# Moving 280 stores and transfers from ScalarE's DMA queue to the sync engine's

## The chip, the cores and the metric

The kernel runs on one core of one Trainium2 chip. The metric is device time in microseconds (us) of one execution. A core has TensorE (PE, the matrix products), VectorE (DVE), ScalarE (ACT), GpSimd (POOL) and the sync engine (SP), each with its own stream of instructions, and 16 DMA engines that all streams share. A DMA is issued by an instruction in the stream of one of SP, ACT or POOL; that instruction waits, in its place in the stream, for whatever its data need, and what stands behind it in the stream waits too.

## The reference, cut to what matters

```python
def reference(x, p, ...):                       # x (1, 2048, 1024), p (1, 1, 2048, 256)
    z = rms_norm(x, mix_norm_g) @ w_in          # 1024 -> 26 * 128 columns
    y_conv = short_conv_mixer(z[..., :1536], conv_mix_w)
    y_rwkv = rwkv7_mixer(z[..., 1536:], ...)
    x = x + concatenate([y_conv, y_rwkv]) @ w_out
    x = x + conv_glu_ffn(rms_norm(x, ffn_norm_g), ...)      # 1024 -> 2 * 2816 -> 1024
    e = rms_norm(p @ ple_w_proj, ple_norm_g)
    gate = sigmoid(rms_norm(x, ple_gate_norm_g) @ ple_w_gate)
    return rms_norm(x + gate * e, final_norm_g)

def wkv7_scan(r, w, k, v, kk, a):               # per head, S is 64 x 64
    # S_t = S_{t-1} diag(w_t) + (S_{t-1} (-kk_t)) (kk_t*a_t)^T + v_t k_t^T,  out_t = S_t r_t
```

The recurrence of `wkv7_scan` runs over all 2048 frames. The kernel works it out by chunks of 64 frames, and for each chunk a unit lower triangular matrix has to be inverted, which is called the solve below.

## The kernel before

Time is cut into four groups (g) of 512 frames. First come the input projections of all four groups, to about 720 us; then for each group the output projection (o), the ConvFFN (up with line 417 behind it, down with line 457), the embedding (e, `ple_embed`, in the middle of the up products) and the gate products, with the final norm of the group behind the first rows of the next. Each product is made of three matmuls of split halves (hi and lo) over blocks of 128 x 512, accumulated in three PSUM buffers.

A weight comes from the host as raw float32 (`raw`, issued by SP) only once. ACT writes its hi half (line 153), POOL its lo half (line 154), and SP stores the split pair to DRAM (line 171, names k..., such as ku). Later groups load the kept pair by a DMA that POOL issues (line 161). There are four buffers for split pairs (whl...), so a load is issued just when a pair has been used up.

The time mixer (RWKV) runs beside the products as 16 units (u = 0 to 15) of 128 frames each: a generator that a product step advances by one. TensorE's instructions keep the order in which the program writes them; the other engines' orders, and SP's, are set by a scheduler that simulates the program and puts ready instructions in the order of its clock, with priority for some. A unit's input is z of its frames: the projections store it to `zs` (line 308) and the unit loads it from there (tw, ad, gd, k, v, r, lines 563 to 568, on SP). A solve has these steps: DVE transposes the triangular blocks into `ltt` (line 763); four DMAs store them to a DRAM tile `ld` (768); four DMAs read them back in another layout into `lm` (775), where each waits for all of `ld`; DVE folds two rows into one (`fold`, lines 783 to 786); POOL clears two diagonals (787, 788); DVE does 16 steps of substitution (794, 798); one DMA stores the result to `xd` (803); four DMAs read it into `dt` (810); DVE transposes it into `dn` (814), POOL copies it into `tT` (821, `tt` in the profile). TensorE uses `dn` first in `gm_ps`, some twenty product steps after the solve began. `xs` is loaded with the identity for the solve (790).

Other transfers: y, e, p, x and xr are rows that SP loads (line 203); the conv's result goes to `ys` at line 336, the unit's at line 931, e to `es` at line 371, and the output at line 519. The buffers u, yc, e, o and others share one pool with six buffers (`buf`, tag b); a buffer is free when the store from it has landed. All DMAs that SP and ACT issue share eight completion semaphores in turn.

Of the kernel before, what the change touches and what calls it, by code (L numbers as in the profile page):

```python
# [62 lines left out]
def tile_trunk(  # L63
# [18 lines left out]
    nc = tc.nc  # L82
# [37 lines left out]
    def v(name, i, n=1):  # L120
        o, _ = VEC[name]
        return vec[:, o + i : o + i + n]
# [25 lines left out]
    zs = [dram.tile([P, 14, G], F32, tag=f"zs{g}", name=f"zs{g}") for g in range(NG)]  # L148
    ys = [dram.tile([P, 8, G], F32, tag=f"ys{g}", name=f"ys{g}") for g in range(NG)]
    es = [dram.tile([P, 8, G], F32, tag=f"es{g}", name=f"es{g}") for g in range(NG)]  # L150
# [26 lines left out]
    def weight(pools, src, name):  # L177
        return [
            half(pools, src[:, 512 * c : 512 * c + 512], f"{name}_{c}", f"{name}_{c}")
            for c in range(2)  # L180
        ]

    def quad(pools, src, mp, name):
        cols = slice(256 * mp, 256 * mp + 256)
        return [half(pools, src[:, :, cols].rearrange("j p c -> p j c"), name, name)]
# [12 lines left out]
    def buf(pools, name):  # L198
        return pools["tmp"].tile([P, G], F32, tag="b", name=name, bufs=NBUF)
# [53 lines left out]
    def scaled(pools, ps, rstd, halo, pad):  # L253
        zb = pools["tmp"].tile([P, G + 2], F32, tag="zb", name="zb")
        nc.vector.tensor_tensor(out=zb[:, 2 : G + 2], in0=ps, in1=rstd, op=ALU.mult)  # L255
        nc.gpsimd.tensor_copy(zb[:, 2 - pad : 2], halo)
        nc.gpsimd.tensor_copy(halo, zb[:, G + 2 - pad : G + 2])
        return zb
# [10 lines left out]
    def product(pools, w, rows, evac):  # L269
        ps = pools["psd"].tile([P, G], F32, tag="d", name="ps_mm")  # L270
        for k in range(KD):
            mm3(ps, w, k, rows.hs[k], k == 0, k == KD - 1)
            if k == 3:
                yield
        if rows.ss is None or rows.scale is not None:
            with tc.high_priority():
                evac(ps, rows.scale)
        else:
            with tc.high_priority():
                raw = buf(pools, "raw")  # L280
                nc.scalar.copy(raw, ps)
            rows.held.append((raw, evac))
            if len(rows.held) == HELD:
                rows.scale = rows.ss.rstd(pools)
                with tc.high_priority():
                    for raw, evac in rows.held:
                        evac(raw, rows.scale)
        yield
# [6 lines left out]
    def in_proj(pools, g, rows, nxt):  # L295
        def project(m, evac):
            return product(pools, weight(pools, w_in[m], f"in{m}"), rows, evac)

        def lerp(j):
            def evac(ps, rstd):  # L300
                zb = scaled(pools, ps, rstd, z_last[:, j : j + 1], 1)
                u = buf(pools, "u")
                nc.scalar.activation(u, zb[:, 2 : G + 2], AF.Copy, scale=mu_c[:, j : j + 1])
                nc.vector.scalar_tensor_tensor(
                    out=u, in0=zb[:, 1 : G + 1], scalar=v("rwkv_mu", j), in1=u,
                    op0=ALU.mult, op1=ALU.add,
                )
                nc.scalar.dma_start(out=zs[g][:, j, :], in_=u)
            return evac

        for j in (12, 0, 4, 8, 13, 1, 5, 9, 2, 6, 10, 3, 7, 11):
            yield from project(12 + j, lerp(j))

        for i in range(4):
            st = {}

            def evac_x(ps, rstd):
                x = st["x"] = buf(pools, "xin")
                nc.vector.tensor_tensor(out=x, in0=ps, in1=rstd, op=ALU.mult)
                nc.vector.tensor_tensor(out=x, in0=x, in1=rstd, op=ALU.mult)  # L320

            def evac_c(ps, rstd):
                t = scaled(pools, ps, st["x"], cx_last[:, i, :], 2)
                u = st["c"] = buf(pools, "cu")
                nc.scalar.activation(u, t[:, 2 : G + 2], AF.Copy, scale=v("conv_mix_w", 8 + i))
                for d in (1, 0):
                    nc.vector.scalar_tensor_tensor(
                        out=u, in0=t[:, d : d + G], scalar=v("conv_mix_w", 4 * d + i), in1=u,
                        op0=ALU.mult, op1=ALU.add,
                    )  # L330

            def evac_b(ps, rstd):
                u = buf(pools, "yc")
                nc.vector.tensor_tensor(out=u, in0=ps, in1=rstd, op=ALU.mult)
                nc.vector.tensor_tensor(out=u, in0=u, in1=st["c"], op=ALU.mult)
                nc.scalar.dma_start(out=ys[g][:, i, :], in_=u)

            if i:
                nxt(3 * i - 3)
            yield from project(i, evac_x)  # L340
            if i:
                nxt(3 * i - 2)
            yield from project(8 + i, evac_c)
            if i:
                nxt(3 * i - 1)
            yield from project(4 + i, evac_b)

    def ple_rows(pools, g):
# [9 lines left out]
    def ple_embed(pools, g, st):  # L358
        hs = st
        ss = SumSq()  # L360
        for mp in range(KD // 2):
            w = quad(pools, w_proj, mp, f"pj{mp}")
            for mm in range(2):
                m = 2 * mp + mm
                ps = pools["psd"].tile([P, G], F32, tag="d", name="ps_e")
                for k in range(2):
                    mm3(ps, w, 2 * k + mm, hs[k], k == 0, k == 1)
                with tc.high_priority():
                    t = buf(pools, "e")
                    nc.scalar.copy(t, ps)  # L370
                    nc.scalar.dma_start(out=es[g][:, m, :], in_=t)
                ss.add(pools, t)
            yield
        embed[g] = ss
# [12 lines left out]
    def dense_rest(pools, g, yrows, nxt):  # L387
        tmp = pools["tmp"]
        gs = slice(g * G, (g + 1) * G)
# [120 lines left out]
        def finish():  # L510
            rstd = ss.rstd(pools)
            with tc.high_priority():
                for m in range(KD):
                    t = buf(pools, "o")
                    nc.vector.scalar_tensor_tensor(
                        out=t, in0=x2[m], scalar=v("final_norm_g", m), in1=rstd,
                        op0=ALU.mult, op1=ALU.mult,
                    )
                    nc.scalar.dma_start(out=out[m, :, gs], in_=t)

        pending.append(finish)

# [54 lines left out]
    def rwkv_unit(rp, S, u, loaded, following):  # L577
        pr, ch, ps_p, ps_c = rp["prep"], rp["chain"], rp["ps_p"], rp["ps_c"]
        g, off = u // 4, (u % 4) * P
        s = 0  # L580
        ts = slice(off, off + P)
# [16 lines left out]
        def r8(t):  # L598
            return t.rearrange("p (h n) -> p h n", h=8)
# [23 lines left out]
        for ct in range(4):  # L623
# [3 lines left out]
            out=ksum, in_=ps_n.rearrange("p (a h n) -> p a h n", a=4, h=2),  # L627
# [12 lines left out]
        for ct in range(4):  # L640
# [3 lines left out]
            out=mean, in_=r8(ps_v), op=ALU.add, axis=mybir.AxisListType.X  # L644
# [4 lines left out]
        for c in range(2):  # L649
            rs = slice(64 * c, 64 * c + 64)  # L650
            pair = []
            for par in range(2):
                t = ch.tile([P, 4, 64], F32, tag=f"suv{par}", name=f"suv{par}_{u}_{c}")
                vr = slice(64 - 64 * par, 128 - 64 * par)
                nc.vector.scalar_tensor_tensor(
                    out=t[vr], in0=mean4[rs, :, par, None].broadcast_to([64, 4, 64]),
# [29 lines left out]
        def cv(t):  # L686
# [9 lines left out]
            out=b_t, in0=tha, scalar=1.0, in1=kr, op0=ALU.add, op1=ALU.mult  # L696
        )
        b4 = cv(b_t)
        for rs, cs in ((E, lo), (O, hi)):
            nc.vector.scalar_tensor_tensor(  # L700
                out=bk[rs, :, :, cs], in0=b4[rs], scalar=0.5, in1=em[rs, :, :, 1:65],
# [63 lines left out]
        )  # L765
        for pq in range(4):
            q = pq % 2
            nc.scalar.dma_start(
                out=ld[pq].rearrange("c a i j -> i c a j"),
                in_=ltt[32 * pq : 32 * pq + 32, :, :, 32 * q : 32 * q + 32],  # L770
            )
        lm = ch.tile([P, 32, 32], F32, tag="lm", name=f"lm{u}", bufs=1)
        for r in range(4):
            eng = nc.sync if r % 2 else nc.scalar
            eng.dma_start(
                out=lm[r:P:4].rearrange("m i j -> m (i j)"),
                in_=ld.rearrange("q c a i j -> (q c a) (i j)"),
            )
# [12 lines left out]
        for i in range(0, 32, 2):  # L791
# [3 lines left out]
                out=pd[:, :, :, 0:n], in0=xs[:, :, None, 0:n].broadcast_to([P, 8, 2, n]),  # L795
# [3 lines left out]
                out=xs[:, :, i : i + 2], in_=pd[:, :, :, 0:n], op=ALU.add,  # L799
# [4 lines left out]
            out=xd.rearrange("q n r c i -> (q n r) (c i)"),  # L804
            in_=xs.rearrange("p c i -> p (c i)"),
        )
        dt_ = ch.tile([P, 8, 32], F32, tag="dt", name=f"dt{u}", bufs=1)
        for pq in range(4):
            eng = nc.sync if pq % 2 else nc.scalar
            eng.dma_start(  # L810
                out=dt_[32 * pq : 32 * pq + 32], in_=xd[pq].rearrange("n r c i -> (r c) n i")
            )
# [110 lines left out]
        yt = big("yt")  # L923
# [4 lines left out]
            )  # L928
        hi_tt(out=yt, in0=yt, in1=v_t, op=ALU.add)
        hi_tt(out=yt, in0=yt, in1=g_t, op=ALU.mult)  # L930
        nc.scalar.dma_start(out=ys[g][:, 4:8, ts], in_=yt)
        yield

    pools, rp = {}, {}
# [139 lines left out]
```

## Time and profile before

| | |
|---|---|
| median of 3 runs | 2907.62 us (2907.26 to 2908.49) |
| profiled execution | 2908.45 us, its span 2906.5 us |
| mean granted clock of TensorE | 0.984 of full speed |
| busy: PE, DVE, ACT, POOL | 2768.1, 1908.3, 959.9, 1117.4 us |
| DMA queue of POOL (q0), SP (q1), ACT (q10): share of 16 engines' span | 39.4%, 24.0%, 5.2% |

A busy time is the sum over the instructions of an engine; the share of the span that it leaves is idle, and the trace names for each idle time the instruction or the DMA whose end released it. An issue of a DMA (SPq, ACTq) isn't counted as busy, but the time that it takes and the time that it waits hold up what stands behind it on that engine. A row `[2.06 <-DMA whld<-kd]` behind an instruction says that its engine stood idle for 2.06 us before it and that the DMA from kd to whld released it.

### The profile page before, as it was taken

How to read it: one execution, taken by the hardware profiler on the slowest of the kernel's cores; microseconds unless marked ns; L12 is line 12 of the kernel's file. 1: busy time of each engine (PE TensorE's matmuls, PEld its weight loads, DVE VectorE, ACT ScalarE, POOL GpSimd, SP SyncE). 2: the span in 40 equal slices, each digit the busy share in tenths (PEclk: the TensorE clock that was granted, in tenths of full speed). 3: DMA queues.
4: the chain of work that ended last, by engine and by line, in shares of the span. 5: the costliest groups of instructions: out<-in, count | busy, mean ns of one | idle time of the engine just before them, and what ended most of it. 6: DMA issues, size and time to landing. Idle time of an engine off the chain costs nothing.

```text
span 2906.5 us, 42153 instructions
## 1 busy us (share of the span) xinstructions
PE 2768.1 (95%) x15464; PEld 2226.7 (77%) x15464; DVE 1908.3 (66%) x3039; ACT 959.9 (33%) x1721; POOL 1117.4 (38%) x1700
## 2 busy tenths in 40 slices
PE   8999999999889999989999999999999999999997
PEld 5778888778677877767778887777788877788885
DVE  5575665648587868796766676857676765544446
ACT  5332232312553433443412223434222143411113
POOL 4533232324556565652333333333333332433221
PEclk9999999999999999989999999999999999999998
DMA  8887777767777777767666565766565668666665
GB/s 298 297 261 217 236 214 223 209 210 243 263 252 245 258 241 247 248 228 230 178 186 185 173 192 172 233 202 200 174 192 169 187 187 266 216 195 189 196 188 169
DMA packets 285802, 629.95 MB, mean 217 GB/s; under 512 B 60186, under 2 KB 113690, under 8 KB 285596
## 3 DMA queue, kind: packets, MB, share of 16 engines
q0 software_dynamic: 95040, 346.07, 39.4%
q1 hardware_dynamic: 134144, 232.83, 24.0%
q10 hardware_dynamic: 56412, 48.36, 5.2%
q8 instruction: 122, 2.00, 0.3%
q14 instruction: 84, 0.69, 0.1%
HBM read 467.77 MB, written 159.38 MB: 216 GB/s over the span
## 4 chain that ended last, share of the span: by engine, by line
PE 50%; DVE 22%; DMA 14%; issue 6%; ACT 5%; POOL 3%; ACTq 1%; SPq 0%; DVEq 0%; POOLq 0%
PE ps_mm L86 33%; PE ps_d L86 11%; DVE uf L417 3%; DVE pd L794 3%; DVE xs L798 2%; DMA lm<-ld 1%; DMA xd<-xs 1%; DMA ld<-ltt 1%; DVE zb L255 1%; DVE sq L229 1%; DMA es<-e 1%; PE o_ps L86 1%; DMA dt<-xd 1%; DVE lo L215 1%; DMA x<-in_xT 1%
## 5 line engine op out<-in xcount | busy, mean ns | idle before, releaser
L86 PE MATMUL ps_mm<-hi,whlu 128*128 128x512 f32 x2816 | 910.6, 397 | 11.3 <-POOL whlu L154 5.1
L86 PEld LDWEIGHTS ps_mm<-hi,whlu 128*128 128x128 f32 x2816 | 532.3, 189 | 131.9 <-POOL whlu L154 7.8
L86 PE MATMUL ps_mm<-hi,whlin 128*128 128x512 f32 x1664 | 542.9, 400 | 19.6 <-ACT whlin L153 7.1
L86 PE MATMUL ps_mm<-lo,whlu 128*128 128x512 f32 x1408 | 552.3, 392 | 1.5 <-DVE lo L215 1.5
L86 PE MATMUL ps_d<-hi,whld 128*128 128x512 f32 x1408 | 456.1, 396 | 16.7 <-DMA whld<-kd 7.2
L86 PEld LDWEIGHTS ps_mm<-hi,whlin 128*128 128x128 f32 x1664 | 316.7, 190 | 93.0 <-ACT whlin L153 7.1
L417 DVE SCALAR_TENSOR_TENSOR uf<-zb,vec,uf 128x512 f32<-128x512 f32 x352 | 298.6, 851 | 89.6 <-ACT uf L412 78.4
L86 PE MATMUL ps_mm<-lo,whlin 128*128 128x512 f32 x832 | 328.9, 395 | 2.8 <-DVE lo L215 2.8
L412 ACT ACTIVATE uf<-zb,vec 128x512 f32<-128x512 f32 x176 | 143.1, 815 | 562.0 <-DVE zb L255 536.8
L86 PEld LDWEIGHTS ps_d<-hi,whld 128*128 128x128 f32 x1408 | 265.6, 189 | 79.2 <-DVE x L457 8.4
L86 PEld LDWEIGHTS ps_mm<-lo,whlu 128*128 128x128 f32 x1408 | 266.8, 189 | 56.2 <-DVE lo L215 2.4
L161 POOL DMA_DIRECT2D whlu<-ku x264 | 141.7, 537 | 436.8 <-PE ps_mm L86 289.1
L255 DVE TENSOR_TENSOR zb<-ps_mm,rstd 128x512 f32<-128x512 f32 x216 | 148.5, 688 | 208.0 <-PE ps_mm L86 204.4
L86 PE MATMUL ps_d<-lo,whld 128*128 128x512 f32 x704 | 275.4, 391 | 0.0
L457 DVE TENSOR_TENSOR x<-ps_d,x 128x512 f32<-128x512 f32 x192 | 131.6, 687 | 139.5 <-PE ps_d L86 138.7
L86 PEld LDWEIGHTS ps_mm<-lo,whlin 128*128 128x128 f32 x832 | 158.4, 190 | 38.1 <-DVE lo L215 6.6
L161 POOL DMA_DIRECT2D whlin<-kin x156 | 84.1, 539 | 248.9 <-PE ps_mm L86 207.7
L86 PE MATMUL ps_mm<-hi,whlg 128*128 128x512 f32 x512 | 169.2, 406 | 3.4 <-DMA whlg<-kg 3.4
L86 PE MATMUL ps_mm<-hi,whlo 128*128 128x512 f32 x512 | 163.1, 397 | 8.5 <-DMA whlo<-ko 4.9
L154 POOL TENSOR_TENSOR lo<-th,hi 128x512 fp32r<-128x512 f32 x88 | 115.2, 1310 | 110.9 <-ACT hi L153 110.3
L154 POOL TENSOR_TENSOR whlu<-rawu,whlu 128x512 fp32r<-128x512 f32 x88 | 122.6, 1398 | 88.9 <-ACT whlu L153 79.2
L86 PEld LDWEIGHTS ps_d<-lo,whld 128*128 128x128 f32 x704 | 133.2, 189 | 26.0
(205 smaller groups left out, 4248.0 us busy)
## 6 DMA issues: line engine op xcount, KB each, us to landing
whlu<-ku POOLq DMA_DIRECT2D x264, 512.0 KB, 4.5
whlin<-kin POOLq DMA_DIRECT2D x156, 512.0 KB, 4.8
whld<-kd POOLq DMA_DIRECT2D x132, 512.0 KB, 4.0
ku<-whlu SPq DMA_DIRECT2D x88, 512.0 KB, 4.7
kin<-whlin SPq DMA_DIRECT2D x52, 512.0 KB, 5.3
whlo<-ko POOLq DMA_DIRECT2D x48, 512.0 KB, 5.5
whlg<-kg POOLq DMA_DIRECT2D x48, 512.0 KB, 3.9
rawu<-in_w_up SPq DMA_DIRECT2D x88, 256.0 KB, 4.1
```

The source lines that it names most:

```text
L86: return pin(nc.tensor.matmul(*args, **kw))
L154: nc.gpsimd.tensor_tensor(out=lo, in0=raw, in1=hi.bitcast(F32), op=ALU.subtract)
L161: nc.gpsimd.dma_start(out=t, in_=kept[key])
L215: nc.vector.scalar_tensor_tensor(out=lo, in0=src, scalar=gcol, in1=hi.bitcast(F32), op0=ALU.mult, op1=ALU.subtract)
L229: nc.vector.tensor_tensor(out=sq, in0=sq, in1=self.acc, op=ALU.add)
L255: nc.vector.tensor_tensor(out=zb[:, 2 : G + 2], in0=ps, in1=rstd, op=ALU.mult)
L412: nc.scalar.activation(u, zb[:, 2 : G + 2], AF.Identity, bias=v("ffn_conv_b", n), scale=v("ffn_conv_w", 88 + n),)
L417: nc.vector.scalar_tensor_tensor(out=u, in0=zb[:, d : d + G], scalar=v("ffn_conv_w", 44 * d + n), in1=u, op0=ALU.mult, op1=ALU.add,)
L457: nc.vector.tensor_tensor(out=x2[m], in0=ps, in1=x2[m], op=ALU.add)
L794: tt(out=pd[:, :, :, 0:n], in0=xs[:, :, None, 0:n].broadcast_to([P, 8, 2, n]), in1=lm[:, None, i : i + 2, 0:n].broadcast_to([P, 8, 2, n]), ...
L798: nc.vector.tensor_reduce(out=xs[:, :, i : i + 2], in_=pd[:, :, :, 0:n], op=ALU.add, axis=mybir.AxisListType.X,)
```

## The change

Seven places of the kernel issue their DMAs from `nc.sync` instead of `nc.scalar`; nothing else is edited. Where the four transfers of `lm` and of `dt` alternated between the two engines, all four are SP's.

```diff
@@ lerp (zs), evac_b (ys), ple_embed (es), finish (out), end of a unit (ys)
-                nc.scalar.dma_start(out=zs[g][:, j, :], in_=u)
+                nc.sync.dma_start(out=zs[g][:, j, :], in_=u)
...
-                nc.scalar.dma_start(out=ys[g][:, i, :], in_=u)
+                nc.sync.dma_start(out=ys[g][:, i, :], in_=u)
...
-                    nc.scalar.dma_start(out=es[g][:, m, :], in_=t)
+                    nc.sync.dma_start(out=es[g][:, m, :], in_=t)
...
-                    nc.scalar.dma_start(out=out[m, :, gs], in_=t)
+                    nc.sync.dma_start(out=out[m, :, gs], in_=t)
...
-        nc.scalar.dma_start(out=ys[g][:, 4:8, ts], in_=yt)
+        nc.sync.dma_start(out=ys[g][:, 4:8, ts], in_=yt)
@@ the solve
         for pq in range(4):
             q = pq % 2
-            nc.scalar.dma_start(
+            nc.sync.dma_start(
                 out=ld[pq].rearrange("c a i j -> i c a j"),
...
         for r in range(4):
-            eng = nc.sync if r % 2 else nc.scalar
+            eng = nc.sync
             eng.dma_start(
                 out=lm[r:P:4].rearrange("m i j -> m (i j)"),
...
         for pq in range(4):
-            eng = nc.sync if pq % 2 else nc.scalar
+            eng = nc.sync
             eng.dma_start(
                 out=dt_[32 * pq : 32 * pq + 32], in_=xd[pq].rearrange("n r c i -> (r c) n i")
```

The scheduler then orders SP and ACT anew. TensorE's order stays, POOL's nearly so; DVE's moves by a few places within each solve. Three places follow.

In unit 7, where first-pass weights are still being split, ACT before the change has two `lm` transfers among its casts of weights (whlu18 is the pair of half 18, hi written from rawu18):

```order
L768 DMA ld7_10522<-ltt7_10523 32x8x32 x4
L153 CAST whlu18_0_10708<-rawu18_0_10709 128x512
L775 DMA lm7_10529<-ld7_10522 32x1024
L153 CAST whlu18_1_10715<-rawu18_1_10716 128x512
L775 DMA lm7_10529<-ld7_10522 32x1024
L153 CAST whlu40_0_10755<-rawu40_0_10756 128x512
```

and after it the casts alone:

```order
L757 COPY tok7_1_10499<-ps_k_10510 128x512
L153 CAST whlu18_0_10708<-rawu18_0_10709 128x512
L153 CAST whlu18_1_10715<-rawu18_1_10716 128x512
L153 CAST whlu40_0_10755<-rawu40_0_10756 128x512
L153 CAST whlu40_1_10762<-rawu40_1_10763 128x512
```

The casts moved up to the place where `ld7` and `lm7` stood. SP in the same place has before the change the two other `lm` transfers, and then raw loads and stores of kept pairs:

```order
L775 DMA lm7_10529<-ld7_10522 32x1024 x2
L168 DMA rawu19_0_10811<-in_w_up 128x512
L171 DMA ku18_0_10713<-whlu18_0_10708 128x1024
L168 DMA rawu19_1_10818<-in_w_up 128x512
L171 DMA ku18_1_10720<-whlu18_1_10715 128x1024
L168 DMA rawu41_0_10858<-in_w_up 128x512
```

and after it

```order
L768 DMA ld7_10522<-ltt7_10523 32x8x32 x4
L775 DMA lm7_10529<-ld7_10522 32x1024 x2
L168 DMA rawu19_0_10811<-in_w_up 128x512
L775 DMA lm7_10529<-ld7_10522 32x1024
L168 DMA rawu19_1_10818<-in_w_up 128x512
L775 DMA lm7_10529<-ld7_10522 32x1024
L171 DMA ku18_0_10713<-whlu18_0_10708 128x1024
L171 DMA ku18_1_10720<-whlu18_1_10715 128x1024
L168 DMA rawu41_0_10858<-in_w_up 128x512
```

Four `ld` and four `lm` stand in one row with two raw loads between the last three `lm`; the store ku18_0 comes behind them. In unit 12, SP has before the change:

```order
L203 DMA e_17309<-es1_103 128x512
L203 DMA y_17347<-ys2_100 128x512
L203 DMA e_17355<-es1_103 128x512
L775 DMA lm12_17184<-ld12_17177 32x1024 x2
L203 DMA xr_17394<-in_xT 128x512
L203 DMA xr_17433<-in_xT 128x512
L203 DMA xr_17508<-in_xT 128x512
```

and after it

```order
L203 DMA e_17309<-es1_103 128x512
L203 DMA y_17347<-ys2_100 128x512
L768 DMA ld12_17177<-ltt12_17178 32x8x32 x4
L203 DMA e_17355<-es1_103 128x512
L775 DMA lm12_17184<-ld12_17177 32x1024
L203 DMA xr_17394<-in_xT 128x512
L775 DMA lm12_17184<-ld12_17177 32x1024 x3
L203 DMA xr_17433<-in_xT 128x512
L203 DMA xr_17508<-in_xT 128x512
```

One load of e moved between `ld12` and `lm12`, and one of xr between the first `lm12` and the other three. At the end of the same solve SP had `dt` on both sides of a load of p:

```order
L203 DMA p_18050<-in_pT 128x512
L803 DMA xd12_17245<-xs12_17195 128x256
L810 DMA dt12_17247<-xd12_17245 32x8x32
L203 DMA p_18056<-in_pT 128x512
L810 DMA dt12_17247<-xd12_17245 32x8x32
L203 DMA y_21854<-ys3_101 128x512
L790 DMA xs13_18604<-in_c_tri 128x256
```

and now has

```order
L203 DMA p_18050<-in_pT 128x512
L803 DMA xd12_17245<-xs12_17195 128x256
L203 DMA p_18056<-in_pT 128x512
L810 DMA dt12_17247<-xd12_17245 32x8x32 x4
L203 DMA y_21854<-ys3_101 128x512
L790 DMA xs13_18604<-in_c_tri 128x256
```

so that the load of p stands ahead of all four `dt`.

## Rows read from the trace of the kernel before

**Rows 1.** The page's first part: busy us, share of the span, instructions

```profile
PE 2768.1 (95%) x15464; PEld 2226.7 (77%) x15464; DVE 1908.3 (66%) x3039; ACT 959.9 (33%) x1721; POOL 1117.4 (38%) x1700
```

**Rows 2.** The waits of TensorE: releaser, us in total, times, longest

```profile
PE ps_mm L86 <- ACT hi L214: 7.8, 6, 3.1
PE ps_d L86 <- DMA whld<-kd: 7.2, 5, 2.1
...
PE ps_b L86 <- ACT tok L757: 4.7, 2, 3.5
...
PE ps_e L86 <- ACT tok L757: 4.0, 3, 2.7
```

**Rows 3.** Line 775 (lm): issue ns min/median/max; who waited, us, times

```profile
L775 ACTq DMA_DIRECT2D lm<-ld x32: 456/493/950, 157.8 to 2280.3; - x32
...
  DVE fold L783: 41.2, 11
```

**Rows 4.** Line 810 (dt), the same columns

```profile
L810 ACTq DMA_DIRECT2D dt<-xd x32: 309/384/782, 202.3 to 2320.2; - x32
...
  DVE dn L814: 67.6, 16
  POOL tt L821: 62.1, 20
```

**Rows 5.** Line 371 (es)

```profile
L371 ACTq DMA_DIRECT2D es<-e x32: 326/326/345, 800.9 to 2515.4; - x32
```

**Rows 6.** Line 768 (ld)

```profile
L768 ACTq DMA_DIRECT2D ld<-ltt x64: 309/462/1189, 152.6 to 2275.5; - x64
```

**Rows 7.** Timeline of unit 9: start us, us, instruction, [idle before it <-releaser]

```profile
1455.65 1.11 SPq L775 DMA_DIRECT2D lm<-ld  x2
...
1456.19 0.62 ACT L153 CAST hi<-th 128x512 fp32r<-128x512 f32 x1 [3.76 <-DMA ld<-ltt]
...
1456.22 0.81 ACTq L775 DMA_DIRECT2D lm<-ld  x1
...
1459.59 0.69 DVE L783 TENSOR_TENSOR fold<-lm,c_sq 128x512 f32<-128x512 f32 x1 [0.84 <-DMA lm<-ld]
...
1462.34 0.15 POOL L787 MEMSET lm<- 128x32 f32 x1 [3.03 <-DVE lm L786]
...
1462.81 0.53 POOL L161 DMA_DIRECT2D whld<-kd  x1 [0.28 <-PE ps_d L86]
...
1466.65 0.50 PE L86 MATMUL ps_d<-hi,whld 128*128 128x512 f32 x1 [2.06 <-DMA whld<-kd]
```

**Rows 8.** Timeline of unit 7, ACT, POOL and SP

```profile
1131.30 0.62 ACT L153 CAST whlu<-rawu 128x512 fp32r<-128x512 f32 x1 [5.96 <-DMA ld<-ltt]
...
1132.00 1.29 POOL L154 TENSOR_TENSOR whlu<-rawu,whlu 128x512 fp32r<-128x512 f32 x1 [6.78 <-DMA ld<-ltt]
...
1136.34 0.33 SPq L168 DMA_DIRECT2D rawu<-in_w_up  x1
```

**Rows 9.** Timeline of TensorE, 1164 to 1188 us

```profile
1164.28 0.73 PE L86 MATMUL ps_mm<-hi,whlu 128*128 128x512 f32 x2 [0.49 <-POOL whlu L154]
...
1187.57 0.73 PE L86 MATMUL ps_d<-hi,whld 128*128 128x512 f32 x2 [1.01 <-POOL whld L154]
```

**Rows 10.** Timeline of TensorE in unit 13

```profile
2031.28 0.50 PE L86 MATMUL ps_d<-hi,whld 128*128 128x512 f32 x1 [1.96 <-DMA whld<-kd]
```

**Rows 11.** Timeline of unit 12 behind its solve

```profile
1913.77 0.42 SPq L810 DMA_DIRECT2D dt<-xd  x1
...
1917.58 0.45 DVE L814 STREAM_TRANSPOSE dn<-dt 128x256 f32<-128x256 f32 x1 [2.19 <-DMA dt<-xd]
...
1919.93 0.50 PE L86 MATMUL ps_mm<-hi,whlu 128*128 128x512 f32 x1 [3.12 <-ACT hi L214]
```

**Rows 12.** Windows of TensorE: from:to, us, busy, granted clock, DMA share, GB/s

```profile
1467.20:1470.60 3.40, 3.40 (x9) 0.50 0.53 180
...
1921.20:1924.60 3.40, 3.40 (x39) 0.50 1.07 361
```

## The prediction

> **What bounds the kernel now.** I read the busy table first: TensorE works 2768.1 of the span's 2906.5 us, ScalarE (ACT) 959.9 [rows 1]. So 138 us, start and tail among them, is all that any order of DMAs could return, and a change pays or costs only where a TensorE gap grows or shrinks. Next the table of waits for TensorE: no DMA that the change moves stands in it. What the change could touch there are waits for ACT (hi 7.8, tok 4.7 and 4.0 us) and for kept weights that arrive late (whld 7.2 us) [rows 2]. The moved DMAs reach TensorE only at one remove: a solve transfer is late, VectorE (DVE) or GpSimd (POOL) stands, and a weight behind it on POOL is late. Then the answers for single lines, where those waits have sums: the fold of the solve waited 41.2 us in 11 units for lm, the transpose dn 67.6 us for dt, the copies into tt on POOL 62.1 us [rows 3, 4]. Last the timelines, for which of these waits have a TensorE gap behind them.
>
> **What the change removes.** Of the issues, 280 leave ACT: 56 zs, 16 ys of the conv, 32 es, 32 out, 64 ld, 32 lm, 32 dt, 16 ys of a unit. With 0.33 us for the 136 stores of zs, ys, es and out [rows 5], 0.46 for ld [rows 6], 0.49 for lm [rows 3] and 0.38 for dt and for the unit's ys [rows 4] this is 45 + 29 + 16 + 12 + 6 = 108 us of ACT's issue time. ACT idles 1947 us of the span anyway, so I price it at nothing by itself. Its waits are worth more. An lm issue waits on ACT for ld to land, and what stands behind it waits too: in unit 9 the cast of hi stood 3.76 us so [rows 7], in unit 7 a weight cast 5.96 us and POOL, behind ACT, 6.78 us [rows 8]. Unit 9's wait has no TensorE gap behind it. Unit 7's may: from 1164 to 1188 us TensorE waits five times, 3.8 us in sum, for weights that POOL splits; first and last of the five are shown [rows 9]. ACT free at that place lets POOL begin earlier; I take -3.0 us for it and all smaller ones. Bounds: 0, if POOL is held by the solve instead, and -8, if besides the 3.8 us a quarter of the 16.5 us of hi and tok waits go.
>
> **What it adds: lm.** Before, the four lm transfers go out two by two, SP and ACT at once: SP's two take 1.11 us together from 1455.65, ACT's second starts at 1456.22, 0.57 after the first [rows 7]. Four in a row on SP at about 0.5 us each start up to 1.5 us after the first: the last is 0.95 us later. What does that cost? In unit 9 the fold needs all four; behind the fold comes POOL's memset at 1462.34 after 3.03 us of waiting, behind it on POOL the kept-weight load at 1462.81, and 3.8 us later TensorE goes on after a gap of 2.06 us [rows 7]. The load itself waited another 0.28 us for TensorE, so 0.95 - 0.28 = 0.67 us arrive. Unit 13 has the same rows (gap 1.96 us) [rows 10]: +0.66. In units 8 and 12 ACT's other work had held the last ld back by 1.0 us, which SP gives back; but an e load or an xr load now stands between the four lm (0.35 us), and a norm and a weight wait directly behind the fold: +0.4 and +0.6. In unit 7 two loads of raw weights stand between the lm, the later of which went out at 1136.34 when its buffer was free [rows 8]; the last lm would go out near 1136.7 instead of 1134.6, 2.1 us later, of which the earlier casts give back 0.7: +1.4. Sum +3.7 us. In the other eleven units the fold is later too, but no TensorE gap follows POOL's memset there, or lm was late by ACT already (units 0 and 3); the four half-buffers of kept weights are the cover. If that cover were gone, eleven at 0.95 would add 10 us.
>
> **dt.** Four on SP start 0.38 us apart [rows 4], the last 0.7 us later than in pairs. POOL's copies into tt take 0.45 us each, one after another, and so stay behind the landings: the first copy, on which POOL waits, starts as before. I price POOL at nothing. The transpose dn needs all four. In unit 12 the last dt went out at 1913.77 from SP, dn started at 1917.58 after 2.19 us of waiting, and TensorE went on at 1919.93 after a gap of 3.12 us for hi, which needs what DVE does behind dn [rows 11]; a p load stands before dt there now, so +0.7 us. Elsewhere 0.5 to 12 us lie between dn and the product that uses it; units 14, 5, 4, 1 and 9, where little is left or POOL was short, I give 0.15 + 0.3 + 0.15 + 0.1 + 0.1. Sum +1.5 us. Upper bound: 0.7 in twelve units, 8 us.
>
> **Head of line on SP.** Moved DMAs now queue behind what SP waits for. I put every DMA of SP at its place in the new order and gave it the start that it had in the trace, or the end of its predecessor if that is later. Out of this: zs is late by 0.1 us in the mean, es by 0.1 (0.8 at most), out not at all; the stores of kept weights by 0.2 to 0.4, the loads of k, v and r by 1 us. Six b buffers cover this release of u and yc; the embed phase, which fills them with e and squares, may not quite, and the load of tw follows one es issue more (0.33 us) in two groups. I take +0.8 us, between 0 and 3.
>
> Of the DMA queues the rows show only that an lm issue costs about 0.5 us wherever it is made [rows 3, 7]. Here the Trainium skill speaks for a small effect: its page "DMA: Bandwidth & Descriptors", section "Issuing engines are not separate DMA queues", says that DMAs started from several engines run on the same 16 DMA engines, and that spreading them saves only the sequencers' time; by that the sum below stands as it is. The same page's section "Queues, rings and completion order" says that each DMA engine goes round between the queues that have work; by that one queue would give lm and dt one share instead of two while POOL streams weights, and my estimate would rise by about half of the lm and dt terms, to 2913. No run here shows which holds.
>
> **Sum.** -3.0 + 3.7 + 1.5 + 0.8 = +3.0 us on the profiled execution's 2908.45 us: 2911.4. That execution was 0.8 us over the median of the runs, 2907.62, so 2910.6 us. A difference under 0.2% (5.8 us) can't be told from no change here; the forecast lies inside it.
>
> **Rivals.**
> *Slower, the lm delay reaches TensorE everywhere.* One mechanism: POOL's memset between lm and the weight loads behind it. It decides if the half-buffers are too few in most units, not in five. Price: the 10 us of the eleven other units. A grown gap can also cost the clock: after unit 9's 2.06 us and unit 12's 3.12 us gap the granted clock stood at 0.50 for 3.4 us [rows 12], 1.2 instead of 2.4 GHz, which loses 1.7 us each time. Two thirds of the 10 and two such stretches: 2910.6 + 6.6 + 3.4 = 2920.6. For it: the waits at fold and dn are already waits for these very transfers. Against it: in eleven units no gap follows the memset.
> *Faster, ACT's freedom wins.* With ACT never behind a solve transfer, the -8 of the bound is reached, while lm and dt cost half (+2.6), because ld goes out faster than before. 2907.6 - 8 + 2.6 = 2902, and with two half-clock stretches behind tok gaps gone, 2899. For it: POOL's 6.78 us behind ACT [rows 8]. Against: most of ACT's standing has no TensorE gap behind it.
> *SP becomes the bound.* Raw weights and kept-weight stores behind SP's waits grow later than my replay says, because each feeds the next while weights are first cast (up to 1190 us). Half a microsecond per pair of halves over some 40 pairs: +20, 2928.
> That nothing changes at all, since SP and ACT feed the same DMA engines and ACT has time to spare, gives 2907.6 and lies inside the forecast's case.
>
> **Chances.** Forecast (within 5.8 us either way) 0.43; the lm delay everywhere 0.29; ACT's freedom 0.22; SP the bound 0.06. So faster 0.22, same 0.43, slower 0.35. Range for 8 in 10: 2898, just beyond ACT's freedom with the clock, to 2925, between the two slower cases. The forecast's own range is 2903 to 2914.
>
> **What would show it.** Right: the gaps at units 9 and 13 grow to about 2.7 and 2.6 us, unit 12's to 3.8; the last lm starts 1.5 us after the first in most units; dn's waits grow by about 0.7 in ten units, POOL's for tt hardly; ACT has no more waits for ld and xd; the five gaps from 1164 to 1188 us shrink. Wrong: new gaps for kept weights behind the memset in more than five units (slower), hi and tok gaps gone (faster), casts that wait long for raw loads or kept-weight stores (SP the bound). The greatest doubt is the order of DVE's instructions, which moves a little in every unit and whose effect no row prices.

## The result and the profile after

The changed kernel took 2930.88 us (median of 3 runs, 2925.03 to 2935.12) against 2907.62: a ratio of 1.0070 with a 95% interval of 1.0046 to 1.0095. Measured again later on one chip together with experiments, it was 1.0065 (1.0048 to 1.0081). It is slower, by some 20 us, and lies above the predicted range of 2898 to 2925. Later runs of the kernel before lay between 2901 and 2924 us, so the experiments below are judged by ratios with their intervals.

The first part of the page of the kernel after, its total and its engines:

```profile
span 2929.1 us, 42198 instructions
...
PE 2780.4 (95%) x15464; PEld 2238.0 (76%) x15464; DVE 1906.5 (65%) x3039; ACT 959.6 (33%) x1721; POOL 1109.5 (38%) x1700
```

Beside [rows 1] the span is 22.6 us longer. Of these, 12.3 us are busy time of TensorE for the same 15464 matmuls, and 10.3 us are idle time (2929.1 - 2780.4 = 148.7, before 138.4). More busy time for the same work is the clock: the mean granted clock fell from 0.984 to 0.978. In this trace more than half of the loss is thus not in the gaps but behind them.

Where it comes in is read by comparing the start of each matmul with that of the same matmul before. At 371 us the two kernels are level (-0.3 us), at the end of the input projections (724 us) the new one is 16.5 us behind, at 1648 us 17.8, at 2176 us 22.7 and at the end 23. So three quarters arise between 371 and 724 us, a stretch to which the prediction's sum gave 0.15 us (the dt of unit 4) and whatever part of its 0.8 us for the head of line fell there. Five places make it up, less some small gains, with the shift that each leaves: 393.6 us, +5.9, a gap of 3.37 before ps_g; 477.5, +3.3, a gap of 1.65 for a weight, whose cause was not followed; 546.1, +1.4, a stretch at half clock without a longer gap ahead of it; 563.7, +3.8, a gap of 3.67 before ps_b (1.17 before); 675.3, +5.4, a gap of 3.92 before ps_g. In the sum over the run the waits of TensorE show the first kind (columns: releaser, us in total, times, longest; kernel after):

```profile
PE ps_g L86 <- DVE suv L655: 18.9, 7, 3.9
...
PE ps_d L86 <- DMA whld<-kd: 8.2, 5, 2.1
...
PE ps_b L86 <- ACT tok L757: 5.6, 2, 3.7
```

and, before:

```profile
PE ps_g L86 <- DVE suv L655: 11.1, 8, 3.1
```

`ps_g` and `ps_b` are products of the RWKV units, not of the big matrices. The chain to the first of them, in the timeline of the kernel after (unit 1 ends with its store of ys, line 931; tw is loaded for unit 3, line 564; suv belongs to unit 2):

```profile
383.40 0.37 SPq L931 DMA_DIRECT2D ys<-yt  x1
...
383.86 0.47 SPq L564 DMA_DIRECT2D tw<-zs  x1
...
389.79 0.31 ACT L572 ACTIVATE tw<-tw 64x128 f32<-64x128 f32 x1 [6.11 <-DMA tw<-zs]
390.01 0.71 ACT L303 ACTIVATE u<-zb,mu_c 128x512 f32<-128x512 f32 x1
390.82 0.75 DVE L304 SCALAR_TENSOR_TENSOR u<-zb,vec,u 128x512 f32<-128x512 f32 x1 [3.10 <-ACT u L303]
...
391.60 0.84 DVE L655 SCALAR_TENSOR_TENSOR suv<-mean,ps_v 64x256 f32<-64x256 f32 x2
...
393.59 0.77 PE L86 MATMUL ps_g<-gd,gup 128*128 128x128 f32 x2 [3.37 <-DVE suv L655]
```

and the same place before:

```profile
382.38 0.47 SPq L564 DMA_DIRECT2D tw<-zs  x1
...
383.67 0.38 ACTq L931 DMA_DIRECT2D ys<-yt  x1
...
386.28 0.31 ACT L572 ACTIVATE tw<-tw 64x128 f32<-64x128 f32 x1 [0.97 <-DMA tw<-zs]
...
390.65 0.57 PE L86 MATMUL ps_g<-gd,gup 128*128 128x128 f32 x3 [0.18 <-DVE suv L655]
```

Before, SP issued tw as soon as its buffer was free, 1.3 us before the store went out from ACT. After, the store stands ahead of tw on SP and waits for DVE to finish yt; with the scale moved by -0.3 us, tw goes out 1.8 us later, and its reader starts 5.9 instead of 3.9 us after its issue, behind 256 KB of the store. ACT has tw ahead of the projection's u, so ACT stands 6.11 instead of 0.97 us, DVE's u stands behind ACT's, suv behind DVE's u, and TensorE behind suv. The prediction followed no wait of this chain.

At 563.7 us it is the conv's store (line 336), again in the kernel after:

```profile
547.50 0.32 SPq L336 DMA_DIRECT2D ys<-yc  x1
547.92 0.39 SPq L563 DMA_DIRECT2D k<-zs  x1
...
554.22 0.69 DVE L570 TENSOR_TENSOR kr<-k,vec 128x512 f32<-128x512 f32 x1 [3.57 <-DMA k<-zs]
...
555.00 0.63 ACT L571 ACTIVATE sq<-kr 128x512 f32<-128x512 f32 x1 [2.40 <-DVE kr L570]
...
563.70 0.80 PE L86 MATMUL ps_b<-pbh,hones 128*128 128x512 f32 x1 [3.67 <-ACT tok L757]
```

and before:

```profile
530.38 0.37 SPq L563 DMA_DIRECT2D k<-zs  x1
...
537.76 0.33 ACTq L336 DMA_DIRECT2D ys<-yc  x1
...
550.83 0.50 PE L86 MATMUL ps_b<-pbh,hones 128*128 128x512 f32 x1 [1.17 <-ACT tok L757]
```

The store waits for yc, the load of k behind it goes out 8.7 us later than before, measured from the matmuls around it, and DVE, which before never waited for k (0 of 16 units), stands 3.57 us and ACT 2.40 us.

These three gaps can be looked up in the traces of all the runs below. The two before ps_g are 3.0 to 5.1 us long wherever the unit's store stands on SP ahead of the loads: in both traces of the changed kernel and with the five stores, the stores of zs and ys, or the unit's store alone. They are 0.2 to 0.8 us long wherever that store stays with ACT. The gap before ps_b is 3.7 to 5.5 us long wherever the conv's store is on SP with the loads behind it, and 1.2 us where it stays with ACT.

What follows each gap is in the windows of TensorE (columns as in [rows 12], the granted clock stands behind the count of matmuls):

```profile
392.50:399.30 6.80, 5.71 (x18) 0.50 0.15 53
477.90:481.30 3.40, 3.40 (x10) 0.50 0.85 302
546.10:549.50 3.40, 3.40 (x20) 0.51 1.07 360
563.20:566.60 3.40, 2.90 (x7) 0.50 0.00 0
675.80:679.20 3.40, 3.40 (x12) 0.51 0.74 180
```

At each of the five places the clock goes to 1.2 GHz for 3.4 or 6.8 us; before, it stood at 2.4 GHz through all of 371 to 724 us. Thus the gap of 3.37 us, 3.2 more than before, cost 5.9. At 546.1 us the gaps ahead, 1.20 and 0.26 us, are those of the kernel before; why the clock fell only after the change stays open. In a second trace of the changed kernel the gaps before ps_g and ps_b are 3.38, 5.13 and 5.24 us, each with half clock behind it, and the gap at the weight has none.

The solve's transfers became later by about what was worked out. The answer for line 775 after:

```profile
L775 SPq DMA_DIRECT2D lm<-ld x64: 448/591/2027, 157.0 to 2305.8; - x64
...
  DVE fold L783: 56.4, 11
```

and for line 810:

```profile
  DVE dn L814: 73.2, 15
  POOL tt L821: 64.7, 19
```

Beside [rows 3, 4] the fold waits 15.2 us more in sum, dn 5.6 and tt 2.6 us. Over the 16 units the last lm starts 7.1 us after the transpose ltt, before 6.1, and 2.25 us after the first, before 0.82; ld's last issue gains 0.15 us. From issue to landing lm takes 4.3 us in the median, before 3.9, and dt 3.7, before 3.1, which the sum had left out.

### The profile page after: what moved, and what is told of

The parts are those of the page before. It is cut to its first block, busy times and chain, and to the rows that moved or that the text cites. A ratio compares the mean times of both kernels' runs of the same rounds, so it can differ in the third digit from the quotient of the medians.

```text
span 2929.1 us, 42198 instructions
## 1 busy us (share of the span) xinstructions
PE 2780.4 (95%) x15464; PEld 2238.0 (76%) x15464; DVE 1906.5 (65%) x3039; ACT 959.6 (33%) x1721; POOL 1109.5 (38%) x1700
## 4 chain that ended last, share of the span: by engine, by line
PE 38%; DVE 14%; DMA 9%; issue 4%; ACT 3%; POOL 1%; SPq 1%; DVEq 0%; POOLq 0%; ACTq 0%
PE ps_mm L86 22%; PE ps_d L86 11%; DVE uf L417 3%; DVE pd L794 2%; DMA lm<-ld 1%; DVE xs L798 1%; DMA dt<-xd 1%; DMA ld<-ltt 1%; DMA es<-e 1%; DVE zb L255 1%; DMA y<-ys 1%; DVE x L457 1%; DVE th L430 1%; DVE sq L229 1%; PE o_ps L86 1%
## 5 line engine op out<-in xcount | busy, mean ns | idle before, releaser
L417 DVE SCALAR_TENSOR_TENSOR uf<-zb,vec,uf 128x512 f32<-128x512 f32 x352 | 292.2, 833 | 85.0 <-ACT uf L412 74.0
```

Source lines behind the costliest of these rows:

```text
L417: nc.vector.scalar_tensor_tensor(out=u, in0=zb[:, d : d + G], scalar=v("ffn_conv_w", 44 * d + n), in1=u, op0=ALU.mult, op1=ALU.add,)
```

## The experiments

A ratio is that to the kernel before on the same chip, with its 95% interval. Theory A: stores on SP stand ahead of the units' loads (tw, ad, gd, k, v, r). Theory B: the solve's four transfers one after another.

**Which part.** Stores alone, the solve's transfers alone, the stores of zs and ys alone, lm and dt alone. Each of these kernels makes the named part of the change and leaves the rest as before; the edit of the first is:

```diff
-                nc.scalar.dma_start(out=zs[g][:, j, :], in_=u)
+                nc.sync.dma_start(out=zs[g][:, j, :], in_=u)
... (and lines 336, 371, 519, 931; lines 768 to 810 as before)
```

> Only the five stores (zs, both ys, es, out; 152 DMAs) go from the sync queue, the solve's transfers stay as before. Theory A (head of line: zs and ys stores stand ahead of the loads of tw, k, v, r on the sync queue, those loads come late, the ps_g product waits, and the clock falls behind the gap): about half of the 23 us, 2916 to 2922, with ps_g gaps of 3 us or more near 391 and 659 us of the old time scale. Theory B (the solve's four transfers one after another are the cause): 2905 to 2911, no new ps_g gaps.

Measured: 1.0062 (1.0041 to 1.0083), more than the half of the loss that theory A gave. The stores alone do what the whole change does, and the two gaps before ps_g are there, 3.07 and 5.03 us.

> Only the solve's transfers (ld, lm, dt; 128 DMAs) go from the sync queue, the five stores stay with ScalarE. Theory A: 2910 to 2916, the lm and dt delays of units 9, 12, 13 remain, ps_g as before. Theory B: nearly all of the loss, 2925 to 2931.

Measured: 0.9997 (0.9979 to 1.0016). The range of theory A is 1.0008 to 1.0029 as a ratio, so the interval only reaches its lower part; that of theory B lies far above. B falls.

> Only the stores of zs and of both ys (88 DMAs) go from the sync queue. Theory A: these are the stores ahead of the units' loads, so it takes the same time as all five stores, within 3 us. If es and out carry the loss of the stores: 2905 to 2911.

Measured: 1.0057 (1.0036 to 1.0079), as all five stores: es and out have no part that can be told.

> Only lm and dt (64 DMAs) go from the sync queue, ld stays with ScalarE. If serial issue of lm and dt is what the solve's part costs, at least as slow as with ld moved too: 2910 to 2918, since ld issued back to back is a gain of up to 1 us in units 5, 8 and 12. If ld's move costs (behind the sync engine's waits): 2906 to 2910.

Measured: 1.0048 (1.0028 to 1.0068), above the expected 2910 to 2918, which is 1.0008 to 1.0036. So lm and dt in a row cost when ld stays behind, and nothing that can be told when ld moves too. In this run the last lm starts 7.5 us after ltt and the fold 12.5 us (means over the 16 units), with ld moved too 7.0 and 11.8, before 6.1 and 11.3.

**What is left without them, and single parts.**

> Only ld (64 DMAs) goes from the sync queue; lm and dt stay in pairs on both queues, the five stores with ScalarE. lm and dt alone on the sync queue measured 1.0048, with ld moved too 0.9997. If ld's move is a gain in itself (four issues back to back, ScalarE no longer between them): 0.995 to 0.998. If it only takes back what lm loses: 0.999 to 1.001. If it is a loss (the sync engine's waits ahead of ld): 1.002 or more.

Measured: 1.0019 (1.0009 to 1.0029): no gain by itself, although the last lm starts 5.7 us after ltt and the fold 11.0 us, both a little earlier than before. The parts of the solve don't add up (1.0019, 1.0048, together 0.9997); each edit also moves the order of DVE and POOL a little, and I can't say which of the two makes the difference. This stays open.

> All that the change moves except the stores of zs and of both ys: es, out, ld, lm and dt go from the sync queue. Theory A (zs and ys stores stand ahead of the units' loads): 0.998 to 1.002, and no ps_g gap near 391 and 659 us of the old scale. If es and out cost something of their own beside the solve's transfers: 1.003 to 1.005.

Measured: 1.0010 (0.9996 to 1.0024). The whole change without the stores of zs and ys costs nothing that can be told; ps_g waits 12.6 us in sum.

> Only the 56 stores of zs go from the sync queue. Theory A by store: in the trace of the change the loads of units 3 and 4 stood behind a ys store each, so if the ys stores are what holds them up: within 0.002 of no change. If the zs stores do it by their number: 1.004 or more.

Measured: 1.0014 (1.0000 to 1.0028): 56 stores, little.

> Only the unit's own store of ys (16 DMAs, line 931) goes from the sync queue. Theory A: it stands ahead of the next unit's load of tw and waits for VectorE's last product of the unit; 1.001 to 1.003, with ScalarE's wait for tw longer in unit 3 than before (1.0 us). If the ys stores have no part: within 0.001 of no change.

Measured: 1.0053 (1.0037 to 1.0069), far more than expected: 16 stores are most of the loss. ps_g waits 18.3 us in sum.

> Only the conv's stores of ys (16 DMAs, line 336) go from the sync queue. Theory A: in the trace of the change the load of k of unit 4 stood 8.7 us behind one of them, and VectorE's kr and ScalarE's square waited for it; 1.002 to 1.004, nearly all of it before 720 us, with VectorE waiting for k of units 4 and 5. If the ys stores have no part: within 0.001 of no change.

Measured: 1.0021 (1.0010 to 1.0031). DVE waits 3.8 us for k in unit 4, and the gap before ps_b is 5.35 us.

> All of the change but the 32 stores of ys, which stay with ScalarE. Theory A with the ys stores as its main part: 1.001 to 1.004, kr waits of units 4 and 5 gone. If the loss needs only zs and the solve together: 1.005 to 1.008, as with the change.

Measured: 1.0014 (0.9998 to 1.0030). Without the 32 stores of ys the change is within the noise.

> The changed kernel again, as a measure on the same chip for the three others: 1.005 to 1.009.

Measured: 1.0065 (1.0048 to 1.0081), the changed kernel on this chip.

**Place or queue.** First the six loads of a unit from ACT, in the full change:

```diff
-        nc.sync.dma_start(out=k_t, in_=zs[g][:, 4:8, ts])
+        nc.scalar.dma_start(out=k_t, in_=zs[g][:, 4:8, ts])
... (and tw, ad, gd, v, r)
```

> All of the change, and the six loads of a unit (k, tw, ad, gd, v, r; 96 DMAs) go from ScalarE's queue, so that no store on the sync engine stands ahead of them. Theory A: the loss of the stores goes, 0.999 to 1.003, unless ScalarE's waits ahead of the loads cost as much. If something else than the loads' lateness is the cause: 1.005 to 1.008 as with the change.

Measured: 1.0042 (1.0026 to 1.0059), between the two. It is no clean test: DVE waits 11.8 us for k (7.6 with the change), now in units 11, 14 and 15 too, and one gap before ps_g is still 3.76 us. Then the place alone. The unit's store stays on SP, but is written behind the next loads of tw and ad, and SP keeps that order:

```diff
+    def early(S, u):
+        g, ts = u // 4, slice((u % 4) * P, (u % 4) * P + P)
+        for t, r in ((S["tw"][0], slice(0, 64)), (S["ad"][0], slice(64, 128))):
+            pin(nc.sync.dma_start(out=t[0:64, :], in_=zs[g][r, 12, ts]))
...
         nc.scalar.activation(tha, ps, AF.Tanh, scale=0.5)
+        if u + 1 < 4 * NG:
+            early(S, u + 1)
+        if late:
+            late.pop()()
         yield
...
-        nc.scalar.dma_start(out=ys[g][:, 4:8, ts], in_=yt)
+        late.append(lambda: pin(nc.sync.dma_start(out=ys[g][:, 4:8, ts], in_=yt)))
+        if u + 1 == 4 * NG:
+            late.pop()()
```

> As in the run that moves only the unit's store of ys to the sync queue (1.0053), but the next unit's loads of tw and ad are written ahead of that store and kept in that order, so the store stands one place behind them instead of ahead. Theory A (place on the queue: the loads wait behind a store that waits for VectorE): 0.999 to 1.002, no ps_g gaps of 4 us near 391 and 659 us of the old scale. If the store's queue itself is the cause (its 256 KB share the sync queue with the loads): 1.004 to 1.006 as before.

Measured: 1.0005 (0.9988 to 1.0021), where the same store two places earlier on the same queue was 1.0053 (1.0037 to 1.0069). The rows say it too. With the store ahead of the loads:

```profile
386.32 0.38 SPq L931 DMA_DIRECT2D ys<-yt  x1
...
386.79 0.47 SPq L564 DMA_DIRECT2D tw<-zs  x1
...
393.21 0.31 ACT L572 ACTIVATE tw<-tw 64x128 f32<-64x128 f32 x1 [4.84 <-DMA tw<-zs]
...
397.01 1.25 PE L86 MATMUL ps_g<-gd,gup 128*128 128x128 f32 x5 [3.90 <-DVE suv L655]
```

and behind them:

```profile
388.06 0.47 SPq L558 DMA_DIRECT2D tw<-zs  x1
...
388.95 0.47 SPq L558 DMA_DIRECT2D ad<-zs  x1
...
389.52 0.54 SPq L942 DMA_DIRECT2D ys<-yt  x1
...
391.83 0.31 ACT L579 ACTIVATE tw<-tw 64x128 f32<-64x128 f32 x1 [0.47 <-DMA tw<-zs]
...
396.32 0.91 PE L86 MATMUL ps_g<-gd,gup 128*128 128x128 f32 x6 [0.18 <-DVE suv L666]
```

The time from tw's issue to its use falls from 6.4 to 3.8 us and ps_g's gap from 3.90 to 0.18. The store's data pass over the same queue in both. The place works in two ways at once: ahead of the loads the store holds back tw's issue until DVE has finished yt (measured against the matmuls, 1.8 us), and its 256 KB go out first (2.6 us more from issue to use). No run separates the two.

> All of the change, with tw and ad kept ahead of the unit's store of ys in the same way. Theory A: the part of that store goes (0.5 of 0.65 to 0.7 points), the parts of the conv's store (0.2) and of zs (0.1) stay: 1.002 to 1.004. If the place doesn't matter: 1.006 to 1.007.

Measured: 1.0041 (1.0028 to 1.0054), at the upper edge of what was expected. The conv's stores are still ahead of the loads of k; ps_b waits 9.1 us in sum, ps_g 16.3. The second of the two gaps before ps_g is gone (0.18 us), but the first is still 4.07 us. There the pinned load of tw now stands behind three stores of zs on SP:

```profile
383.27 4.09 SPq L308 DMA_DIRECT2D zs<-u  x3
...
387.45 0.47 SPq L558 DMA_DIRECT2D tw<-zs  x1
...
393.07 0.31 ACT L579 ACTIVATE tw<-tw 64x128 f32<-64x128 f32 x1 [6.82 <-DMA tw<-zs]
...
396.87 1.41 PE L86 MATMUL ps_g<-gd,gup 128*128 128x128 f32 x5 [4.07 <-DVE suv L666]
```

The third of them waited for DVE's u. So it isn't the unit's store as such: another late store ahead of the load makes the same gap.

> The control for both: the kernel before, all stores and the solve on their old queues, with only the loads of tw and ad written earlier and kept in order. No theory expects more than 0.001 either way, since the loads go out at the same place of the sync queue.

Measured: 1.0012 (0.9995 to 1.0029), no difference that can be told. No kernel run here is faster than the one before.

## Why the prediction was wrong

**The step that failed: head of line on SP, taken as +0.8 us, between 0 and 3.** The runs give 1.0062 for the five stores, 18 us, of which the 32 stores of ys make most (1.0053 and 1.0021 alone). For the issues the method was right: every DMA put at its place in SP's new order. Done with the rows of the kernel before, it gives the load of k of unit 4 late by 7.7 us behind the conv's store (measured 8.7) and that of tw of unit 3 by 1.7 us behind the unit's store (measured 1.8). The text kept "the loads of k, v and r by 1 us" and named only the release of buffers as what that could cost. It also left out that a load behind a store's data reaches its reader later after its issue, this tw by 2.0 us. The question left out is who reads the late loads: ACT and DVE, in order, ahead of work for the projections, where TensorE had slack for neither. The sign was in the table of TensorE's waits before: ps_g behind suv stood second in it with 11.1 us, the prediction took up only hi, tok and whld, and ps_g's is the wait that grew most, to 18.9 us.

**The clock, priced only for a rival.** Each of the four longer gaps, of 1.65 to 3.92 us, was followed by a stretch at half clock; over the whole run 12.3 of 22.6 us came as busy time. The price of 1.7 us for 3.4 us was right (the weight's gap of 1.65 us left a shift of 3.3), but belonged to the forecast's own terms too. The share differs from trace to trace: it is 15.5 of 31.9 us in the second trace of the changed kernel, 5.2 of 28.8 with the five stores and 6.2 of 21.8 with the unit's store alone. The trace of the control (loads alone, 1.0012) has 5.2 us more busy time too, so single traces give the size of this part only roughly.

**ACT's freedom, -3.0 us.** ACT's waits for ld and xd, 39.8 us before, are gone, as foretold. Waits for tw rose from 23.8 to 34.0 us, for e's store from 3.0 to 8.8, for out's from 8.2 to 15.4, for the stores of the kept input weights from 7.6 to 14.5. The five gaps between 1164 and 1188 us did not shrink: five in the same work, again 3.8 us in sum. POOL was held by the solve there, as the bound of 0 said: its memset at the fold waited 5.07 us, before 2.61. No gain was seen.

**lm, +3.7, and dt, +1.5 us.** The delay came out as worked out, the last lm 1.0 us later against 0.95, though it starts 2.25 us after the first and not up to 1.5. In unit 13 the gap for the kept weight became 2.13 us in the kernel after:

```profile
2041.24 0.50 PE L86 MATMUL ps_d<-hi,whld 128*128 128x512 f32 x1 [1.55 <-DMA whld<-kd]
...
2047.31 0.50 PE L86 MATMUL ps_d<-hi,whld 128*128 128x512 f32 x1 [1.69 <-DVE zb L255]
...
2051.10 0.54 PE L86 MATMUL ps_d<-hi,whld 128*128 128x512 f32 x1 [2.13 <-DMA whld<-kd]
```

It was to be 2.6 [rows 10], but two more gaps of 1.6 us and the clock came with it, 4.6 us where 0.66 was said. Unit 12's gap of 3.12 us [rows 11] became 1.44 instead of 3.8. In sum the solve alone is 0.9997 (0.9979 to 1.0016), that is -6 to +5 us: the terms -3.0 + 3.7 + 1.5 = +2.2 lie inside, and the single units were not foretold.

**The rivals.** "SP becomes the bound" (0.06) had the right engine and, by luck, nearly the right time, 2928, for the wrong cargo: it named raw weights and kept-weight stores before 1190 us, and it was the units' loads before 724 us. "The lm delay reaches TensorE" (0.29) gave the right sign for a cause that the run with the solve's transfers alone rules out as the main one.

**The rule on issuing engines.** With engine and queue the same, a store's place before or behind two loads is worth 1.0053 against 1.0005. The page "DMA: Bandwidth & Descriptors" of the Trainium skill, section "Issuing engines are not separate DMA queues", says that spreading the issue saves only the sequencers' time. Read as the time to issue, as the prediction read it, that leaves out what decided here: a load behind a store that waits goes out later, and reaches its reader later after that.

## What to carry to other kernels

When a DMA moves to another engine's queue, ask of every load behind its new place: how late does it get at worst, which engine reads it in order, and what for TensorE stands behind that. Take the largest single delays, not the mean, and follow those. A store that waits for a late result belongs behind the loads that are ready, or on another engine's queue, as it was before the change; and a new gap on TensorE is to be priced with the half-clock stretch that may follow it, in the traces named above between a fifth and somewhat over half of the whole loss.

## What was not expected of the hardware

With the unit's store alone on SP, a load of 32 KB (tw) issued 0.47 us behind a store of 256 KB on the same queue reached its reader 6.4 us after its issue; ahead of the store it took 3.8 us. And in the traces after and before the same 15464 matmuls took 2780.4 us instead of 2768.1 at a mean granted clock of 0.978 instead of 0.984.
